# A hybrid attention and S5 step: x normed amid the modulation's loads, and more late turns behind the S5's first carries

## The chip, the cores and the metric

The kernel runs on one core of one Trainium2 chip. Its engines are TensorE (PE, with PEld for the loads of its weights), VectorE (DVE), ScalarE (ACT), GpSimd (POOL) and SyncE (SP), which issues nearly all DMA transfers. The metric is the time of one execution on the device in microseconds (us), less is better. Times of before and after are medians of several runs; a profile is one execution.

## The reference, cut to what matters

One layer works on 1024 prompt tokens and 64 sample tokens of width 1024, 1088 in all, in nine token tiles (eight of 128, one of 64). All is float32.

```
mod   = silu(c) @ w_mod + b_mod                    # c: prompt and sample row
shift, scale, gate = three parts of 1024 columns
h     = rms_norm(x, g_norm) * (1 + scale) + shift
z     = h @ w_in                                   # 4936 columns, split:
q, k, v, qi, ki, wi, ga, u, gs, ma, mb = split_cols(z)
o     = attention of q over the 256 keys that the indexer (qi, ki, wi) selects
y     = S5(u)                                      # complex diagonal scan + D skip
yg    = GLU(gelu(y) @ w_glu)
merged = sigmoid(ma) * ((o * silu(ga)) @ w_attn_proj)
       + sigmoid(mb) * ((yg * silu(gs)) @ w_ssm_proj)
out   = rms_norm(x + gate * (merged @ w_out), g_final)
```

Outputs are `out` for both, the new keys, values and indexer keys, and the S5's last states.

## The kernel before

Products in float32 accuracy are made of float32r halves: a value is cast to `hi` (ACT) and `lo = value - hi` is subtracted (POOL or DVE), and a product is hi·hi + hi·lo + lo·hi, three passes over eight blocks of 128 (`mm3`). `split` (L155) does this for weights that `load_split` loads through two `raw` buffers.

**The start.** silu(c) is turned to columns `scs`. Then the loop at L472 goes through w_mod's first 2048 columns: for each of eight row blocks `k` the tile of the scale half (`j` = 1) and of the shift half (`j` = 0), 128 x 1024 each, 512 KB. `wm` tiles and tiles of x (`load_x`, L459) share one tag with five buffers. `SPLITW` says for each of the sixteen tiles whether it is split (`s`: ACT casts, DVE subtracts, two products with the float32r pair `c4`) or taken in float32 (`d`: one product with `cz`); either way the stationary operand has four columns and the sums land in four partitions of PSUM. x0 is loaded before the last w tile (`X0` = 14), x1 behind it. The steps of the S5's parameters (`ssm_params`, small DVE work) are taken at `PARK`. Then the rows `mrow` are copied out, turned by PE into columns, and DVE forms `acol` (scale) and `shcol` (shift), L510 to L514. The weights `wA` of the first projection (264 columns: three indexer heads, the indexer's keys, its weights) follow in four pairs of row blocks.

`norm(t)` squares a tile of x on ACT with a row sum, POOL takes the power -1/2 (L530), and DVE or ACT scales the tile in place. It also loads x two tiles ahead. `turn_x` (L537) turns one or two tiles by PE into PSUM, applies `acol` and `shcol` on DVE (L552) or ACT (L555), casts to `hhi` on ACT (L558) and subtracts to `hlo` on POOL (L559). `GROUPS` says which tiles go together, `HALVES` how many half groups are turned at each step of the loop over nine tiles (L649), where `chunk_a(t)` projects tile t with `wA`, rotates on POOL (`do_rope`, L239 to L242), stores the indexer's keys and stacks them for the scores. Behind it wB is loaded and the scores, the top-k selection and the attention follow.

**Late work.** The remaining projections are one list of jobs (`products`), 128 columns of w_in each, in three chunks of tokens (`CH`); a job has nine steps. `late` is a generator of these steps, and `weave(main, fill, ratio)` takes `ratio` steps of it for each yield of another stage: the attention (1.15), the S5 (3.2), gelu (3.0). What is left is run behind gelu.

**The S5.** `ssm()` (L1454) yields behind each of its steps: the input products `ssm_in(q)` for four quarters, the scan on DVE, and then for each quarter `ssm_fix(q)` (DVE adds the carries to the quarter's states, L1424 to L1427, and copies them to `zq`, L1435), `ssm_out_tables(q + 1)` (POOL, PE and round trips through DRAM) and `ssm_out(q)` (PE, L1447 and L1448, stored to `y_d`). gelu reads `y_d`, and the GLU follows.

A list scheduler lays out the order within each engine: the program's order is the priority, and an instruction that its model of durations holds for not ready is passed by later ones that are. On the chip each engine and SP's queue run strictly in the order laid out.

Of the kernel before, what the change touches and what calls it, by code (L numbers as in the profile page):

```python
# [51 lines left out]
N_BR = (7, 3, 2)  # L52
R_ATT = 1.15
R_SSM = 3.2
N_GAP = 12
R_GEL = 3.0
N_ATT = 14
# [1 line left out]
QH = 5  # L59
VH = 0  # L60
ORDER = "ost"
GROUPS = ((1, 2), (3, 4), (5, 6), (7,), (8,))
HALVES = (2, 1, 1, 1, 1, 1, 1, 2, 0)
SA = (3, 6, 4, 8, 2, 7, 5)
SB = (6, 3, 4, 8, 5, 2, 7)
MB = 3
PARK = (1, 2, 3)
PAR0 = 2
OT = 5
RAW = 2  # L70
SPLITW = "sdsdsdsdsdsdsddd"
X0 = 14
MODD = (1, 1, 1, 0, 0, 0, 1, 0)
XS_ON = "dadddaddd"
ROPE_ON = {2: "p", 4: "p", 5: "d"}
# [8 lines left out]
def hybrid_step(ctx, tc, ins, outs):  # L84
# [24 lines left out]
    def tpb():  # L109
        return ps_tp.tile([P, 4, P], F32, tag="tp", name="tp")  # L110
# [4 lines left out]
    def big():  # L115
        return ps_big.tile([P, 1024], F32, tag="big", name="big")
# [66 lines left out]
    def load_tok(c0, n):  # L183
        w = tokp.tile([P, 2, KD, n], F32R, tag="wtok", name="wtok")
        src = w_in[:, c0:c0 + n].rearrange("(k p) c -> p k c", p=P)
        nk = 2 if n <= 264 else 1
        for k in range(0, KD, nk):
            load_split(w[:, 0, k:k + nk, :], w[:, 1, k:k + nk, :], src[:, k:k + nk, :])
        return w
# [251 lines left out]
    tp = tpb()  # L441
    pe.transpose(tp[:, 0, :16], crow[0:16], ident[:16, :16])
    for b in range(2):
        silu = act.activation(scs[:, :, b], tp[:, 0, 8 * b:8 * b + 8], AF.Silu)
    c4 = small.tile([P, KD, 4], F32R, name="c4")
    dve.tensor_copy(c4[:, :, 0:2], scs)
    c_rest = dve.tensor_tensor(c4[:, :, 2:4], scs, c4[:, :, 0:2].bitcast(F32), op=OP.subtract)

    def chain(*gens):
        for g in gens:  # L450
            yield from g

    def run(gen):
        for _ in gen:
            pass
# [3 lines left out]
    def load_x(t):  # L459

        xts[t] = sxp.tile([P, D], F32, tag="wm", name="xt", bufs=5)
        sync.dma_start(xts[t][:tok_tile(t)[1]], x_rows(t))


    cz = sxp.tile([P, KD, 4], F32, name="cz", bufs=1)
    pool.memset(cz, 0.0)
    dve.tensor_copy(cz[:, :, 0:2], scs)
    scr = rb.tile([P, 6, 512], F32, tag="t1", name="scr")
    params = ssm_params(ssu)
    next(params)  # L470
    mp = [big(), big()]
    for k in range(KD):  # L472
        for j in (1, 0):
            wm = sxp.tile([P, D], F32, tag="wm", name="wm", bufs=5)
            last_w = sync.dma_start(wm, w_mod[k * P:(k + 1) * P, j * D:(j + 1) * D])
            if SPLITW[(2 * k + 1 - j)] == "d":
                parts = [(cz, wm)]
            else:
                wmh = wpool.tile([P, D], F32R, tag="whi", name="wmh")
                wml = wpool.tile([P, D], F32R, tag="wlo", name="wml")  # L480
                with tc.issue_after(silu.ins), tc.issue_after(c_rest.ins):
                    act.copy(wmh, wm)
                    dve.tensor_tensor(wml, wm, wmh.bitcast(F32), op=OP.subtract)
                parts = [(c4, wmh), (c4, wml)]
            for i, (c, w) in enumerate(parts):
                for h in range(0, D, 512):
                    last_mm[0] = pe.matmul(mp[j][0:4, h:h + 512], c[:, k, :], w[:, h:h + 512],
                              start=(k == 0 and i == 0), stop=(k == KD - 1 and i == len(parts) - 1))
            if 2 * k + 1 - j == X0:
                load_x(0)  # L490
        if k in PARK:
            next(params)
    load_x(1)
    mrow_t = kv1.tile([4, 2, D], F32, tag="bz", name="mrow")
    mrow = [mrow_t[:, i] for i in range(2)]
    for j in (1, 0):
        act.copy(mrow[j][:, 0:512], mp[j][0:4, 0:512])
        dve.tensor_copy(mrow[j][:, 512:], mp[j][0:4, 512:])
    tp = tpb()
    with tc.issue_after(last_mm[0].ins):  # L500
        pe.transpose(tp[:, 1, :40], crow, ident[:40, :40])
    mcol = tp[:, 0, 0:64].rearrange("p (m b) -> p m b", b=4)
    for blk in [*range(8, 16), *range(8)]:
        pe.transpose(mcol[:, blk, :], mrow[blk // 8][:, (blk % 8) * P:(blk % 8 + 1) * P], ident[0:4, 0:4])
    ccol = sxp.tile([P, 3, KD], F32, name="ccol", bufs=1)
    dve.tensor_copy(ccol.rearrange("p a b -> p (a b)"), tp[:, 1, 16:40])
    mc = sxp.tile([P, 16, 4], F32, name="mc", bufs=1)
    dve.tensor_copy(mc, mcol)
    both_b = [ccol[:, i, :, None].to_broadcast([P, KD, 2]) for i in range(3)]
    dve.scalar_tensor_tensor(acol, mc[:, 8:16, 0:2], 1.0, mc[:, 8:16, 2:4], op0=OP.add, op1=OP.add)  # L510
    dve.tensor_tensor(acol, acol, both_b[1], op=OP.add)
    dve.tensor_tensor(acol, acol, both_b[2], op=OP.mult)
    dve.tensor_tensor(shcol, mc[:, 0:8, 0:2], mc[:, 0:8, 2:4], op=OP.add)
    dve.tensor_tensor(shcol, shcol, both_b[0], op=OP.add)  # L514

    with tc.issue_after(last_w.ins):
        wA = load_tok(C_QI + 320, 264)
        load_x(2)
        sync.dma_start(rope, ins["rope_tab"])


    def norm(t):
        nt = tok_tile(t)[1]
        if 0 < t and t + 2 < 9:
            load_x(t + 2)
        xt = xts[t]
        ss = sxp.tile([P, 3], F32, tag="ss", name="ss", bufs=4)
        act.activation(scr[:nt, 4:6].rearrange("p a b -> p (a b)"), xt[:nt], AF.Square, accum_out=ss[:nt, 0:1])
        dve.tensor_scalar(ss[:nt, 1:2], ss[:nt, 0:1], 1.0 / D, EPS, op0=OP.mult, op1=OP.add)
        pool.tensor_tensor(ss[:nt, 2:3], ss[:nt, 1:2], nhalf[:nt], op=OP.pow)  # L530
        if XS_ON[t] == "d":
            dve.tensor_scalar(xt[:nt], xt[:nt], ss[:nt, 2:3], None, op0=OP.mult)
        else:
            act.activation(xt[:nt], xt[:nt], AF.Copy, scale=ss[:nt, 2:3])


    def turn_x(ts):  # L537
# [103 lines left out]
            yield  # L641
    late = counted(products(jobs))
    chunks = [chunk_a(t) for t in range(9)]
    norm(0)
    run(turn_x((0,)))
    norm(1)
    norm(2)
    turns = chain(*[turn_x(g) for g in GROUPS])
    for t in range(9):  # L649
        if t >= PAR0:  # L650
            next(params, None)
        if t < 6:
            norm(t + 3)
        for _ in range(HALVES[t]):
            next(turns)
        next(chunks[t])
        if t:
            next(chunks[t - 1])
# [501 lines left out]
    def gates():  # L1160


        sel = small.tile([P, 2], F32, name="sel")
        for b in range(2):
            dve.tensor_reduce(sel[:, b:b + 1], ident.rearrange("p (g r) -> p g r", r=32)[:, :, b],
                              axis=mybir.AxisListType.X, op=OP.add)
        for h in range(2):
            cols = slice(2 * D + h * 512, 2 * D + h * 512 + 512)
            w = tokp.tile([P, KD, 544], F32, tag="wtok", name="gw")
            pool.memset(w[:, :, 512:], 0.0)  # L1170
            pool.tensor_copy(w[:, :, 512:514], scs)
            sync.dma_start(w[:, :, 0:512], w_mod[:, cols].rearrange("(k p) c -> p k c", p=P))
            yield
            ps = bank1()
            for k in range(KD):
                g = 32 * (k % 4)
                pe.matmul(ps[g:g + 32], w[:, k, 512:], w[:, k, 0:512], start=(k < 4), stop=(k >= 4), skip_group_check=True)
            r = wpool.tile([P, 528], F32, tag="raw", name="grow", bufs=RAW)[:, :512]
            act.copy(r, ps)
            yield  # L1180
            o = bank1()[0:2]
            pe.matmul(o, sel, r, start=True, stop=True)
            act.copy(r[0:2], o)
            bm = wpool.tile([P, 528], F32, tag="raw", name="gbias", bufs=RAW)[0:2, :512]
            sync.dma_start(bm, ins["b_mod"][:, cols].to_broadcast([2, 512]))
            pool.tensor_tensor(bm, r[0:2], bm, op=OP.add)
            sync.dma_start(gate_d[:, h * 512:h * 512 + 512], bm)
# [266 lines left out]
    def ssm():  # L1454
        for q in range(4):
            if q == 0:
                with tc.issue_after(last_mm[0].ins):
                    ssm_in(q)
            else:
                ssm_in(q)  # L1460
            yield
        for i, _ in enumerate(ssm_scan()):
            if i == OT:
                ssm_out_tables(0)
            yield
        for q in range(4):
            ssm_fix(q)
            yield
            if q < 3:
                ssm_out_tables(q + 1)  # L1470
                yield
            ssm_out(q)
            yield
# [228 lines left out]
```

## Time and profile before

| | us |
|---|---|
| three runs, median (lowest to highest) | 1055.84 (1055.79 to 1056.0) |
| the profiled execution | 1058.36 |
| its span, first to last instruction | 1056.6 |
| PE busy | 984.9 |
| DVE busy | 686.0 |
| ACT busy | 462.7 |
| POOL busy | 298.7 |

The span is what the trace covers; the execution's own time is 1.8 us longer. Busy times are sums over the whole span, of stages with different limits. The granted clock of TensorE, 0.968 of full speed on average, is given by stretch: 1.00 is 2.4 GHz, 0.50 is 1.2 GHz.

### The profile page before, as it was taken

The page shows a single profiled execution, that of the slowest core. Times are in us where ns is not written, and L with a number is a line of the kernel's source. Part 1 is how long each engine was busy: PE and PEld are TensorE (multiplying, and loading weights), DVE is VectorE, ACT ScalarE, POOL GpSimd, SP SyncE. Part 2 cuts the span into 40 slices and gives each one's busy share as a digit, 9 for nine tenths or more (in the row PEclk, how much of TensorE's full clock was granted, in tenths as well). Part 3 has the DMA queues.
Part 4 walks back from the last instruction along what each step waited for, and adds up shares of the span by engine and source line. Part 5 has one row for each costly group of instructions (what it writes and reads, how often), then busy time and mean ns, then how long its engine had stood idle before and what let it go on. Part 6 is the DMA issues. An engine that isn't in the chain of part 4 may idle for free. (4 is left out here: it accounts for less than half of the span.)

```text
span 1056.6 us, 16627 instructions
## 1 busy us (share of the span) xinstructions
PE 984.9 (93%) x5948; PEld 893.3 (85%) x5948; DVE 686.0 (65%) x1416; ACT 462.7 (44%) x978; POOL 298.7 (28%) x438
## 2 busy tenths in 40 slices
PE   7777999999899999999999996989979999999997
PEld 1466877998689999999898995879969999998786
DVE  5764898899787778866665999811034556664243
ACT  3574577321276566666625211111462344442122
POOL 2475102531622222112152387351114000001201
PEclk9797999999899999999999998899989999999999
DMA  8730301144332222112294241323733255534133
GB/s 294 230 94 24 91 1 48 44 162 147 83 73 60 59 60 59 51 55 65 60 135 117 83 119 35 85 59 89 189 115 97 83 165 159 161 108 160 50 136 115
DMA packets 137413, 106.18 MB, mean 100 GB/s; under 512 B 32638, under 2 KB 124328, under 8 KB 137328
## 3 DMA queue, kind: packets, MB, share of 16 engines
q1 hardware_dynamic: 135808, 102.82, 34.6%
q10 hardware_dynamic: 1232, 2.23, 0.6%
q8 instruction: 47, 0.77, 0.3%
q14 instruction: 38, 0.31, 0.1%
q0 software_dynamic: 288, 0.05, 0.0%
HBM read 77.79 MB, written 25.17 MB: 97 GB/s over the span
## 5 line engine op out<-in xcount | busy, mean ns | idle before, releaser
L201 PE MATMUL acc<-hhi,whi 128*128 128x384 f32 (+1 forms) x768 | 259.3, 342 | 13.3 <-ACT sg L627 7.4
L202 PE MATMUL acc<-hlo,whi 128*128 128x384 f32 (+1 forms) x768 | 254.3, 335 | 0.0
L157 POOL TENSOR_TENSOR wlo<-raw,whi 128x512 fp32r<-128x512 f32 x64 | 88.2, 1393 | 283.3 <-ACT whi L156 147.8
L201 PEld LDWEIGHTS acc<-hhi,whi 128*128 128x128 f32 x768 | 148.0, 193 | 18.6 <-ACT sg L627 8.0
L206 PE MATMUL acc<-hhi,wlo 128*128 128x384 f32 (+1 forms) x768 | 150.8, 334 | 0.0
L202 PEld LDWEIGHTS acc<-hlo,whi 128*128 128x128 f32 x768 | 148.1, 193 | 0.6
L206 PEld LDWEIGHTS acc<-hhi,wlo 128*128 128x128 f32 x768 | 129.6, 190 | 2.3 <-issue 1.6
L611 ACT COPY st<-acc 128x384 f32<-128x384 f32 (+1 forms) x60 | 27.7, 461 | 102.2 <-PE acc L206 101.7
L1075 DVE TENSOR_TENSOR pt<-tp,pt 128x512 fp32r<-128x512 f32 (+3 forms) x112 | 57.0, 518 | 17.6 <-ACT pt L1074 16.6
L1054 ACT ACTIVATE pm<-pm,mx 128x1024 f32<-128x1024 f32 (+8 forms) x72 | 56.1, 779 | 25.5 <-DVE mx L1047 25.1
L1074 ACT CAST pt<-tp 128x512 fp32r<-128x512 f32 (+3 forms) x112 | 49.3, 451 | 35.9 <-PE tp L1070 34.4
L1637 POOL TENSOR_TENSOR yh<-yh,gfin 128x512 f32<-128x512 f32 (+1 forms) x9 | 11.6, 1291 | 173.3 <-ACT xr L1633 173.3
L1047 DVE CUSTOM_DVE_ANT_0 pm<-sc,bias 128x512 f32<-128x512 f32 (+4 forms) x72 | 42.6, 593 | 26.9 <-PE sc L1044 26.3
L201 PE MATMUL acc<-wohi,mhi 128*128 128x512 f32 (+2 forms) x152 | 56.7, 377 | 0.0
L202 PE MATMUL acc<-wolo,mhi 128*128 128x512 f32 (+2 forms) x152 | 56.7, 377 | 0.0
L1070 PE MATMUL tp<-ident,pm 128*128 128x128 f32 (+2 forms) x328 | 52.8, 270 | 0.7 <-DVE pt L1075 0.6
L1044 PE MATMUL sc<-kst,qs 128*128 128x512 f32 (+3 forms) x192 | 52.0, 352 | 1.1 <-DVE mx L1047 0.5
L156 ACT CAST whi<-raw 128x512 fp32r<-128x512 f32 x64 | 37.8, 618 | 31.9 <-PE acc L202 18.4
L1087 PE MATMUL o<-pt,vst 128*128 128x256 f32 x288 | 47.5, 291 | 1.0 <-DVE pt L1075 1.0
L1070 PEld LDWEIGHTS tp<-ident,pm 128*128 128x128 f32 (+2 forms) x328 | 38.5, 139 | 9.8 <-DVE pt L1075 2.2
L706 DVE SCALAR_TENSOR_TENSOR sc<-relu,wi,sc 128x512 f32<-128x512 f32 (+5 forms) x42 | 42.6, 1017 | 3.8 <-ACT relu L704 1.0
L1087 PEld LDWEIGHTS o<-pt,vst 128*128 128x128 f32 x288 | 39.3, 188 | 4.4 <-DVE pt L1075 3.6
(493 smaller groups left out, 2244.8 us busy)
## 6 DMA issues: line engine op xcount, KB each, us to landing
raw<-in_w_in SPq DMA_DIRECT2D x68, 256.0 KB
wm<-in_w_mod SPq DMA_DIRECT2D x16, 512.0 KB
xt<-in_x_prompt SPq DMA_DIRECT2D x8, 512.0 KB
gw<-in_w_mod SPq DMA_DIRECT2D x2, 2048.0 KB
raw<-in_w_out SPq DMA_DIRECT2D x16, 256.0 KB
xr<-in_x_prompt SPq DMA_DIRECT2D x16, 256.0 KB
ma_d<-st SPq DMA_DIRECT2D x16, 192.0 KB
mb_d<-st SPq DMA_DIRECT2D x16, 192.0 KB
```

The lines of the kernel that those rows point to most:

```text
L157: rest_on[0].tensor_tensor(lo, raw, hi.bitcast(F32), op=OP.subtract)
L201: pe.matmul(ps, lhi(k), rhi(k), start=(k == 0), stop=False)
L202: pe.matmul(ps, lhi(k), rlo(k), start=False, stop=False)
L206: last_mm[0] = pe.matmul(ps, llo(k), rhi(k), start=False, stop=(k == nk - 1))
L706: dve.scalar_tensor_tensor(scores[b][:nq], r[:nq, :n], w, scores[b][:nq], op0=OP.mult, op1=OP.add, accum_out=sums[:nq, 0, col] if h == 4 e ...
L1044: pe.matmul(ps, self.st[:, self.h // 2, self.h % 2, :nq], self.keys[:, self.h // 4, j, c:c + m], start=(j == 0), stop=(j == 1))
L1047: dve.tensor_tensor_reduce(out=self.pm[:, c:c + m], in0=ps, in1=bias[self.b][:nq, c:c + m], op0=OP.add, op1=OP.min, scale=-0.125, scalar=t ...
L1054: act.activation(self.pm, self.pm, AF.Exp, bias=self.ng, scale=-1.0, accum_out=self.sm)
L1070: pe.transpose(tp[:rows, i, :nq], self.pm[:, c0:c0 + rows], ident[:nq, :nq])
L1074: act.copy(d0, tp[:rows, i0:i1, :nq])
L1075: dve.tensor_tensor(d1, tp[:rows, i0:i1, :nq], d0.bitcast(F32), op=OP.subtract)
L1087: last_mm[0] = pe.matmul(o, v[:rows, kt, pr // 2].rearrange("p a d -> p (a d)"), pk[:rows, j, i, :, :nq], start=(kt == 0 and j == 0), stop ...
```

## The change

The modulation's loop goes through all eight tiles of the scale half first, then through the shift half. No tile is split any more: each is taken in float32, with a stationary operand of 32 columns (`scp`), and row block k's sums go to PSUM partitions 32 (k mod 4) and on, so that there are four row groups; `mrow` has 128 partitions, and eight products with the selector `sel` per half (moved here from `gates`) add the groups and turn the rows to columns at once. `acol` is formed in the middle of the loads, `shcol` at the end.

x0 is loaded ahead of all w tiles, x1 to x3 behind w tiles 0, 1 and 2 (`XE`), and wA behind tile 12 (`WA_AT`). These four tiles are normed two tiles later and turned three tiles later, without modulation, into `hraw` (`turn_early`), which takes the buffers of the weights' halves. `mod_early` modulates them in place (per half tile three blocks on DVE, one on ACT), casts and subtracts. x4 to x8 are loaded behind the w tiles without any step of `norm` between, normed at `NORMS` and turned as before in `GROUPS` (4, 5), (6, 7), (8).

In the S5, `ssm_fix(0)` is followed by four yields instead of one (`N_FIX`), so that the weave takes 3 x 3.2 = 9.6 steps of `late` more there.

```diff
+N_FIX = (4, 1, 1, 1)
-GROUPS = ((1, 2), (3, 4), (5, 6), (7,), (8,))
-HALVES = (2, 1, 1, 1, 1, 1, 1, 2, 0)
+XE = (-1, 0, 1, 2)
+WA_AT = 12
+GROUPS = ((4, 5), (6, 7), (8,))
+NORMS = (2, 1, 1, 1, 0, 0, 0, 0, 0)
+HALVES = (0, 1, 1, 1, 1, 1, 1, 0, 0)
-PARK = (1, 2, 3)
+PARK = (3, 5, 7)
-SPLITW = "sdsdsdsdsdsdsddd"
-X0 = 14
...
-    for k in range(KD):
-        for j in (1, 0):
-            wm = sxp.tile([P, D], F32, tag="wm", name="wm", bufs=5)
-            last_w = sync.dma_start(wm, w_mod[k * P:(k + 1) * P, j * D:(j + 1) * D])
-            if SPLITW[(2 * k + 1 - j)] == "d":
-                parts = [(cz, wm)]
-            else:
...
+    hraw = [wpool.tile([P, KD, P], F32, tag=("whi", "wlo")[t % 2], name="hraw") for t in range(len(XE))]
+    def turn_early(t):
+        for k0 in (0, 4):
+            tp = tpb()
+            for i in range(4):
+                pe.transpose(tp[:, i, :], xts[t][:, (k0 + i) * P:(k0 + i + 1) * P], ident)
+            (act.copy if k0 else dve.tensor_copy)(hraw[t][:, k0:k0 + 4], tp)
+    def mod_early(t):
+        c = slice(t * P, (t + 1) * P)
+        for k0 in (0, 4):
+            ks = slice(k0, k0 + 4)
+            for k in range(k0, k0 + 4):
+                if k % 4 < 3:
+                    dve.tensor_scalar(hraw[t][:, k], hraw[t][:, k], acol[:, k, 0:1], shcol[:, k, 0:1],
+                                      op0=OP.mult, op1=OP.add)
+                else:
+                    act.activation(hraw[t][:, k], hraw[t][:, k], AF.Identity, bias=shcol[:, k, 0:1],
+                                   scale=acol[:, k, 0:1])
+            act.copy(hhi[:, ks, c], hraw[t][:, ks])
+            pool.tensor_tensor(hlo[:, ks, c], hraw[t][:, ks], hhi[:, ks, c].bitcast(F32), op=OP.subtract)
...
+    load_x(0)
+    mtp = bank1()
+    mcol = mtp[:, 0:32].rearrange("p (j k b) -> p j k b", j=2, b=2)
+    for n in range(2 * KD):
+        j, k = 1 - n // KD, n % KD
+        wm = sxp.tile([P, D], F32, tag="wm", name="wm", bufs=5)
+        last_w = sync.dma_start(wm, w_mod[k * P:(k + 1) * P, j * D:(j + 1) * D])
+        if n in XE[1:]:
+            load_x(XE.index(n))
+        if n == WA_AT:
+            wA = load_tok(C_QI + 320, 264)
+        g = 32 * (k % 4)
+        for h in range(0, D, 512):
+            last_mm[0] = pe.matmul(mp[j][g:g + 32, h:h + 512], scp[:, k, :], wm[:, h:h + 512],
+                                   start=(k < 4), stop=(k >= 4), skip_group_check=True)
+        if n in PARK:
+            next(params)
+        if n - 2 in XE:
+            norm(XE.index(n - 2))
+        if n - 3 in XE:
+            turn_early(XE.index(n - 3))
+        if k == KD - 1:
+            act.copy(mrow[:, j, 0:512], mp[j][:, 0:512])
+            dve.tensor_copy(mrow[:, j, 512:], mp[j][:, 512:])
...
+                for b in range(KD):
+                    pe.matmul(mcol[:, j, b, :], mrow[:, j, b * P:(b + 1) * P], sel, start=True, stop=True)
...
+    load_x(NE)
+    with tc.issue_after(last_w.ins):
+        load_x(NE + 1)
+        sync.dma_start(rope, ins["rope_tab"])
+        for t in range(NE + 2, 9):
+            load_x(t)
...
-    norm(0)
-    run(turn_x((0,)))
-    norm(1)
-    norm(2)
+    for t in range(2):
+        mod_early(t)
...
-        if t < 6:
-            norm(t + 3)
+        if t + 2 < NE:
+            mod_early(t + 2)
+        for _ in range(NORMS[t]):
+            norm(todo.pop(0))
...
             ssm_fix(q)
-            yield
+            for _ in range(N_FIX[q]):
+                yield
```

## Rows read from the trace of the kernel before

**Rows 1.** The page: busy time by engine (share of the span) x instructions.
```profile
PE 984.9 (93%) x5948; PEld 893.3 (85%) x5948; DVE 686.0 (65%) x1416; ACT 462.7 (44%) x978; POOL 298.7 (28%) x438
```

**Rows 2.** Stretches: length, each engine's busy time (x instructions), clock, DMA share, GB/s.
```profile
39.30:98.70 59.40, 44.17 (x296) 40.11 (x294) 32.20 (x69) 38.10 (x84) 43.71 (x148) 0.84 0.33 91
650.30:662.70 12.40, 0.07 (x2) 0.05 (x1) 12.31 (x14) 0.00 (x0) 10.06 (x7) 0.63 0.00 1
662.70:668.40 5.70, 5.70 (x31) 5.70 (x31) 5.63 (x12) 1.00 (x2) 0.00 (x0) 0.61 0.01 3
```

**Rows 3.** Stretches, a slice of the loads of w_mod; same columns.
```profile
20.00:30.00 10.00, 10.00 (x28) 1.26 (x27) 9.52 (x56) 2.30 (x4) 0.61 (x3) 1.00 0.94 342
```

**Rows 4.** Timeline, loads issued on SP: start, duration, engine, line, op, tiles, count.
```profile
1.54 22.78 SPq L475 DMA_DIRECT2D wm<-in_w_mod  x15
7.60 0.33 SPq L475 DMA_DIRECT2D wm<-in_w_mod  x1
27.01 0.33 SPq L475 DMA_DIRECT2D wm<-in_w_mod  x1
66.29 1.28 SPq L462 DMA_DIRECT2D xt<-in_x_sample  x1
```

**Rows 5.** Timeline, PE: one row group, turns, four row groups, the next product.
```profile
12.85 1.88 PE L487 MATMUL big<-wm,cz 128*4 128x512 f32 x4
38.96 1.92 PE L547 MATMUL big<-ident,xt 128*128 128x128 f32 x8 [0.48 <-ACT xt L534]
253.65 1.92 PE L1177 MATMUL tp<-gw 128*32 128x512 f32 x16
255.51 0.44 PE L201 MATMUL acc<-hhi,whi 128*128 128x384 f32 x1
```

**Rows 6.** Timeline, other engines of the start, up to the last rope.
```profile
5.27 1.04 ACT L482 CAST wmh<-wm 128x1024 fp32r<-128x1024 f32 x1 [2.00 <-DMA wm<-in_w_mod]
32.82 0.67 DVE L498 COPY mrow<-big 4x512 f32<-4x512 f32 x1
33.20 1.06 ACT L528 ACTIVATE scr<-xt 128x1024 f32<-128x1024 f32 x1
39.28 0.18 DVE L512 TENSOR_TENSOR acol<-acol,ccol 128x16 f32<-128x16 f32 x1
98.42 0.24 POOL L242 TENSOR_TENSOR zA<-rope,rope 64x32 f32<-64x32 f32 x1
```

**Rows 7.** Groups by line, POOL, 39.3 to 98.7: busy, mean ns | idle, releaser.
```profile
L530 POOL TENSOR_TENSOR ss<-ss,nhalf 128x1 f32<-128x1 f32 (+1 forms) x7 | 4.6, 658 | 6.4 <-DVE ss L529 6.4
L157 POOL TENSOR_TENSOR wtok<-raw,wtok 128x528 fp32r<-128x528 f32 x3 | 4.3, 1455 | 0.5 <-ACT wtok L156 0.5
```

**Rows 8.** Waits of PE: total, times, longest.
```profile
PE tp L1448 <- DVE zq L1435: 12.3, 1, 12.3
```

**Rows 9.** Timeline, PE: the product behind that wait.
```profile
662.65 0.82 PE L1448 MATMUL tp<-zq,cs 128*128 128x136 f32 x2 [12.33 <-DVE zq L1435]
```

**Rows 10.** Timeline, DVE: the same 544-wide form beside POOL's work and without it.
```profile
649.34 1.77 DVE L1424 TENSOR_TENSOR f<-car,arf 128x544 f32<-128x544 f32 x1
663.74 0.72 DVE L1424 TENSOR_TENSOR f<-car,arf 128x544 f32<-128x544 f32 x1
```

**Rows 11.** Timeline, ACT: evictions of one late job's three chunks.
```profile
735.40 0.49 ACT L627 ACTIVATE sg<-acc 128x384 f32<-128x384 f32 x1 [3.38 <-PE acc L206]
739.61 0.49 ACT L627 ACTIVATE sg<-acc 128x384 f32<-128x384 f32 x1 [3.72 <-PE acc L206]
743.13 0.44 ACT L627 ACTIVATE sg<-acc 128x320 f32<-128x320 f32 x1 [3.02 <-PE acc L206]
```

**Rows 12.** Timeline, POOL: a late job's product beside DVE.
```profile
672.05 1.44 POOL L620 TENSOR_TENSOR oT<-sg,oT 128x384 f32<-128x384 f32 x1 [11.29 <-ACT sg L619]
```

**Rows 13.** Timeline, the tail: the last gelu's rest, the last late chunk's eviction.
```profile
779.87 1.29 DVE L1503 TENSOR_TENSOR glo<-gt,ghi 128x1088 fp32r<-128x1088 f32 x1
807.75 0.43 ACT L611 COPY st<-acc 128x320 f32<-128x320 f32 x1
```

More of the change, by code (lines that the diff above doesn't have):

```diff
@@ L443, in hybrid_step @@
     for b in range(2):
[L444 to L447, printed above, removed]
+        act.activation(scs[:, :, b], tp[:, 0, 8 * b:8 * b + 8], AF.Silu)
     def chain(*gens):
@@ L462, in load_x @@
         sync.dma_start(xts[t][:tok_tile(t)[1]], x_rows(t))
[L465 to L471, printed above, removed]
-    for k in range(KD):
-        for j in (1, 0):
-            wm = sxp.tile([P, D], F32, tag="wm", name="wm", bufs=5)
-            last_w = sync.dma_start(wm, w_mod[k * P:(k + 1) * P, j * D:(j + 1) * D])
-            if SPLITW[(2 * k + 1 - j)] == "d":
-                parts = [(cz, wm)]
-            else:
[L479 to L519, printed above, removed]
     def norm(t):
         nt = tok_tile(t)[1]
-        if 0 < t and t + 2 < 9:
-            load_x(t + 2)
         xt = xts[t]
@@ new lines, in hybrid_step @@
+    scp = sxp.tile([P, KD, 32], F32, name="scp", bufs=1)
+    pool.memset(scp, 0.0)
+    dve.tensor_copy(scp[:, :, 0:2], scs)
+    sel = small.tile([P, 2], F32, name="sel")
+    for b in range(2):
+        dve.tensor_reduce(sel[:, b:b + 1], ident.rearrange("p (g r) -> p g r", r=32)[:, :, b],
+                          axis=mybir.AxisListType.X, op=OP.add)
+    scr = rb.tile([P, 6, 512], F32, tag="t1", name="scr")
+    params = ssm_params(ssu)
+    next(params)
+    load_x(0)
+    mp = [big(), big()]
@@ new lines, in hybrid_step @@
+    mrow = kv1.tile([P, 2, D], F32, tag="bz", name="mrow")
+    mtp = bank1()
[13 more added lines that the diff above has]
+        if n in PARK:
+            next(params)
+        if n - 2 in XE:
[5 more added lines that the diff above has]
+            dve.tensor_copy(mrow[:, j, 512:], mp[j][:, 512:])
+            with tc.issue_after(last_mm[0].ins):
+                if j:
+                    pe.transpose(mtp[:, 64:104], crow, ident[:40, :40])
+                for b in range(KD):
+                    pe.matmul(mcol[:, j, b, :], mrow[:, j, b * P:(b + 1) * P], sel, start=True, stop=True)
+            if j:
+                ccol = sxp.tile([P, 3, KD], F32, name="ccol", bufs=1)
+                dve.tensor_copy(ccol.rearrange("p a b -> p (a b)"), mtp[:, 80:104])
+                both_b = [ccol[:, i, :, None].to_broadcast([P, KD, 2]) for i in range(3)]
+                dve.scalar_tensor_tensor(acol, mcol[:, 1], 1.0, both_b[1], op0=OP.add, op1=OP.add)
+                dve.tensor_tensor(acol, acol, both_b[2], op=OP.mult)
+            else:
+                dve.tensor_tensor(shcol, mcol[:, 0], both_b[0], op=OP.add)
@@ L537, in turn_x @@
+    NE = len(XE)
+    load_x(NE)
[4 more added lines that the diff above has]
+            load_x(t)
     def turn_x(ts):
@@ L643, in hybrid_step @@
     chunks = [chunk_a(t) for t in range(9)]
-    norm(0)
-    run(turn_x((0,)))
-    norm(1)
-    norm(2)
+    for t in range(2):
+        mod_early(t)
     turns = chain(*[turn_x(g) for g in GROUPS])
+    todo = list(range(NE, 9))
     for t in range(9):
@@ L1160, in gates @@
     def gates():
[L1163 to L1166, printed above, removed]
         for h in range(2):
```

## The prediction

> **What bounds the kernel now.** I read the page's busy times first: TensorE (PE) is busy 93% of the span [rows 1], so only a stretch in which PE stands idle or runs at half clock can give much. The list of PE's waits and its timeline name the one large hole: 12.33 us up to 662.65, in which the S5's output products wait for DVE's carries [rows 8, 9]. The stretches, engine by engine [rows 2], show the other place: from 39.3 to 98.7, where x is normed, turned, modulated and first projected, PE is busy 44.2 of 59.4 us at a granted clock of 0.84, and no engine is full (POOL 43.7, the others less). Before 39.3 the modulation's products follow their loads. From 98.7 on PE is nearly dense, so time won ahead of it, or in the hole, moves the whole rest forward. The profiled execution took 1058.36 us, 1.8 more than its span; the three timed runs have a median of 1055.84, 2.5 below it. I make the sum as a difference on the profiled execution and take it off the median.
>
> **The start, until the shift column.** Four tiles of x enter the five buffers that w_mod's sixteen tiles run through: 20 loads up to the last w tile (17 before, where x0 stood ahead of it), and wA's four stand ahead of the last three.
> - Before, the sixth load was issued at 7.60 and the seventeenth at 27.01 [rows 4]: eleven intervals of 1.76 us. The wire's share of one is 0.52 MB at 342 GB/s [rows 3], 1.53. The twentieth is then issued at 7.60 + 14 x 1.53 to 1.76 = 29.0 to 32.2; wA's 1.08 MB (264 x 1024 x 4 B) adds 3.2 at that rate: 32.2 to 35.4.
> - Behind the last issue: 3.7 to land (issued 1.54, ACT released by it at 5.27 [rows 4, 6]), four float32 records 1.9 [rows 5], the PSUM copy 0.7 [rows 6], eight products with sel, one vector op 0.2. No row shows a sel product. The nearest are eight turns, 1.92 at half clock [rows 5]: bounds are half of it, 1.0, and twice it, 3.8 (two records each); I take 1.5, as they move two columns instead of 128. Sum 8.0: shift column at 40.2 to 43.4.
> - Holding: an x tile keeps its buffer through square 1.1, pow 0.7, scale 0.7, eight turns 1.9 and their copies 0.7 [rows 5 to 7] (the scale taken as the copy), 5.1 us against a w tile's 1.9. Four such over five buffers cost at most 4 x 3.2 / 5 = 2.5; I take half. Queued behind it: SP is a queue, so each w load stands behind the x load that waits for a buffer, and wA's third and fourth raw loads, which wait for ACT's and POOL's splits, hold the last three w loads; on PE the next w product stands behind turns whose tile is not yet scaled.
> - So 44.6, with bounds 39.7 (sel 1.0) and 49.9 (43.4 + 2.5 + 2.3 for dear sel products + 14 x 0.12, should each w tile cost PE its whole 1.88). Before it was 39.28 [rows 6]: the change costs 5 us here.
>
> Seven w tiles lose their split into two float32r halves, a cast of 1.04 on ACT [rows 6] and a subtraction on DVE, for which a w buffer and PE had waited; what that leaves free on both carries the four norms, hraw's copies and sel's two reductions. The four row groups: the same form in gates ran 16 records in 1.92 us against 4 in 1.88 for one group [rows 5], so PE stops setting the interval. The parameters stay at the same w tiles.
>
> A rule against it: the Trainium skill (TensorEngine Tiling (Array Packing), Key Properties) says that changing the tiling mode drains TensorE, and the new loop alternates narrow products with full-width turns. In the trace gates' sixteen narrow records run from 253.65 to 255.57 and the next full-width product starts at 255.51 [rows 5]: no drain is seen. By the rule some ten switches would each cost a fraction of a microsecond, by the row nothing; either lies inside the holding term.
>
> **The start, from the shift column to the last projected tile.** It lasted 59.4 us, to POOL's last rope at 98.66 [rows 6]. POOL's 43.7 in it lose three of wA's subtractions (3 x 1.46) and two pows (2 x 0.66) [rows 7], now done earlier: 38.0; its hlo subtractions, ropes and constants stay. 15.7 us of it were idle, behind casts and behind norms strung on late loads: the last x tile was issued at 66.29 [rows 4], because x tiles waited for buffers. After the change all five are free when x4 to x8 are wanted, and four tiles need only modulation, cast and subtraction. Lower bound: 38.0 + 2 to the first cast = 40. Upper: all idle time stays, 53.7. I take 46, half the idle time, since cast and subtraction still alternate half tile by half tile.
> So 44.6 + 46 = 90.6 against 98.7: -8.1, with bounds -19.0 (39.7 + 40) and +4.9 (49.9 + 53.7). What is late next: wB's loads, which stand on SP behind the last key store; they move along.
>
> **The S5.** Three yields more at 3.2 steps each put 9.6 steps of the late projections between the first carries and the first output products. A chunk's pace is 4.21 us at 384 columns and 3.52 at 320 [rows 11], a job of nine steps 11.9: 1.33 a step, 12.7 for 9.6. Their weights come by loads that nothing in the hole delays. The hole is 12.3 [rows 8]. The output products behind it ran 5.7 us at clock 0.61 [rows 2]; at full clock 3.5, so 2.2 more.
> Against: a job's splits and products come along on POOL, 2 x 1.46 [rows 7] and 3 x 1.44 [rows 12], 7.2 us. DVE's 544-wide ops took 0.72 where POOL stood idle and 1.77 where it was busy 10 of 12.4 us [rows 2, 10], so up to 7.2 x 0.59 = 4.2 us of delay for the carries, of which the fill's excess covers 0.4. Gain between 14.5 and 10.7; I take 12. It is zero if the turns don't go there. What the late work covers later is thinner: its last chunk is evicted at 807.75, the last gelu's rest ends at 781.2 [rows 13], so 26 us of it lie behind gelu, of which 12.7 are taken; the cover holds.
>
> **Sum.** -8.1 - 12 = -20.1: 1038.3 for a profiled execution, 1035.7 against the median.
>
> **Rivals.**
> 1. The start gives nothing: POOL's idle time stays, since cast and subtraction follow each other through one tile at a time (for it: POOL idles 15.7 us with much of its data on chip). Then 44.6 + 53.7 = 98.3, -0.4, and only the S5 counts: 1043.4. Against: a good part of that idle time ended with late norms. Chance 0.17.
> 2. The S5's gain is given back in the tail, where gelu then sets the end of the stage. For: ACT evicts late chunks behind gelus that wait for their loads. Against: the 26 us of cover. Then -8.1 alone: 1047.7. Chance 0.08.
> 3. Slower: the five buffers starve the loads. Every w load stands in SP's queue behind x tiles that give their buffer back only when PE, in order, has turned them, and PE stands behind w products that wait for loads. Price: 14 us for each microsecond of interval. All gains outside it are 13.4 (59.4 - 46) + 12 = 25.4, so it decides from a shift column at 64.7, which is an interval of 3.3 (18.8 + 14 x 3.3). At 3.6 the column comes at 69.2 and the kernel takes 1055.8 + 29.9 - 25.4 = 1060.3. Against: 1.76 was kept while ACT and DVE split w tiles. Chance 0.06.
> 4. No change: the order within each queue is laid out anew, and a hole as long opens elsewhere. 1055, chance 0.04.
>
> **How the numbers follow.** The forecast has 0.65 and a range of its own of 1025 to 1045. To hold 0.8 the range takes in rivals 1 and 2 and both bounds of the start: 1022.3 (-19.0 - 14.5) to 1052 (+4.9 with 8.7 left of the S5's gain). 0.2%, about what a measurement can tell from no change, is 2.1 us. Faster: forecast and rivals 1 and 2, 0.90, less a little for their mixtures, 0.89; same 0.04; slower 0.07.
>
> **What the profile after would show.** Loads: w's last issue near 35 and the shift column's vector op near 44; past 50 the holding term failed. POOL's last rope near 91, its idle time between shift column and that near 8, and all x loads issued by 50. In the S5: PE's wait for zq under 4 us, the clock there full, late products between. In the tail: the last late chunk evicted near 788, still behind the last gelu. A wait for gelu ahead of the GLU's products would make rival 2 right, w loads more than 3 us apart rival 3; a stage of 54 us behind the shift column rival 1.

## The result, and the profile after

The changed kernel takes 1043.01 us (median of 4 runs, 1042.34 to 1043.72) beside 1055.82 for the kernel before; the ratio is 0.9887 [0.9864, 0.9909]. That is 12.8 us faster, where 20.1 were forecast. The time lies inside the range, but it is made up otherwise than forecast: the new start loses time, and the S5's turns gain nearly twice what they were given. The profiled execution took 1043.72 us with a span of 1041.9; PE is busy for 982.1 of it (before: 984.9 [rows 1]).

The waits of TensorE (PE) after: total, times, longest. L469, L527 and so on are lines of the changed file, some 20 beyond those of before.

```profile
PE big L527 <- DVE par L367: 8.2, 1, 8.2
PE big L571 <- DVE xt L472: 6.6, 3, 4.2
PE tp L613 <- POOL zA L244: 6.4, 3, 4.1
PE tp L1469 <- DVE zq L1456: 5.5, 1, 5.5
```

The 12.3 us in front of the S5's output products [rows 8] are gone, and 5.5 stand in front of the second quarter's. New are 8.2 us in front of the first product of the modulation and 6.6 for the scaled tiles of x; 4.1 of the 6.4 us for zA are one wait near the end of the start (before it was 3.9).

**The start.** The timeline of the changed kernel: ScalarE (ACT) and PE ahead of the first product, two loads of w_mod on SP (the sixth of the loads that share the five buffers, and the last), the products with the last tile, and the ends of the two stages that the forecast dated.

```profile
0.74 1.28 ACT L468 ACT_TABLE_LOAD   x1 [0.74 <-PEq L1711]
5.18 1.06 ACT L468 ACTIVATE scr<-xt 128x1024 f32<-128x1024 f32 x1 [3.16 <-DMA xt<-in_x_prompt]
8.02 1.06 ACT L468 ACTIVATE scr<-xt 128x1024 f32<-128x1024 f32 x1 [1.70 <-DMA xt<-in_x_prompt]
9.19 1.28 ACT L446 ACT_TABLE_LOAD   x1
10.48 0.25 ACT L446 ACTIVATE scs<-tp 128x8 f32<-128x8 f32 x2
11.07 1.93 PE L527 MATMUL big<-wm,scp 128*32 128x512 f32 x4 [8.17 <-DVE par L367]
...
14.72 0.34 SPq L520 DMA_DIRECT2D wm<-in_w_mod  x1
...
40.54 0.33 SPq L520 DMA_DIRECT2D wm<-in_w_mod  x1
...
46.29 1.90 PE L527 MATMUL big<-wm,scp 128*32 128x512 f32 x4 [0.29 <-DMA wm<-in_w_mod]
51.05 0.17 DVE L550 TENSOR_TENSOR shcol<-tp,ccol 128x16 f32<-128x16 f32 x1 [1.50 <-PE tp L542]
106.28 0.24 POOL L244 TENSOR_TENSOR zA<-rope,rope 64x32 f32<-64x32 f32 x1
109.83 0.80 PE L718 MATMUL big<-kis,qsa 128*128 128x512 f32 x1
```

And the row of before that answers to the last one, the first product of the index scores:

```profile
102.50 0.80 PE L693 MATMUL big<-kis,qsa 128*128 128x512 f32 x1
```

ACT's queue has the squares of x0 and x1, each waiting for its tile, and a second table load ahead of silu, though the code has silu first. So the first product with w_mod, which needs scp, DVE's copy of silu's output, starts at 11.07 (the lists name a neighbour of that copy on DVE, par), and by then the five buffers have long been full: no load of w_mod is issued until 14.72 (before: 7.60 [rows 4]). The shift column comes at 51.05 (before the last of these vector operations was at 39.28 [rows 6]), the last rope ends at 106.5 (98.66), and the first product of the index scores moves from 102.50 to 109.83: the start is 7.3 us longer.

Stretches after, answering to [rows 2]: shift column to last rope, the time in which the hole was, and 15 us of the carries behind it.

```profile
51.20:106.50 55.30, 40.74 (x272) 38.83 (x272) 32.12 (x78) 32.22 (x73) 38.94 (x145) 0.82 0.21 46
656.60:668.40 11.80, 11.80 (x77) 11.35 (x77) 11.64 (x17) 2.80 (x6) 7.16 (x9) 1.00 0.14 32
672.00:687.00 15.00, 15.00 (x104) 14.55 (x103) 14.90 (x13) 4.52 (x9) 14.69 (x10) 1.00 0.49 105
```

POOL is idle for 16.4 us of the first stretch (55.30 - 38.94); it was 15.7 of 59.4, and 8 were forecast. In the second PE is full at clock 1.00, where it had stood and then run at 0.61. In the third POOL and DVE are both full, and DVE's 544-wide operations behave as in [rows 10], 1.95 us there against 0.72 beside the idle POOL. The last row is the first of the second quarter's copies to zq:

```profile
673.60 1.93 DVE L1445 TENSOR_TENSOR f<-car,arf 128x544 f32<-128x544 f32 x1
678.21 1.95 DVE L1447 TENSOR_TENSOR zs<-zs,f 128x544 f32<-128x544 f32 x1
695.01 0.72 DVE L1448 TENSOR_TENSOR zs<-zs,f 128x544 f32<-128x544 f32 x1
695.99 0.42 DVE L1456 COPY zq<-zs 64x544 f32<-64x544 f32 x1
```

PE waits for these copies until 697.37. The second quarter's carries are added by 673.7, and PE has used the first quarter's zq by 674.7, but on DVE's queue the copies stand behind the sixteen 544-wide operations of the last two quarters (673.60 to 695.73). The order is the same before (there the copies start at 681.41), but no wait of PE hangs on it. So the new wait of 5.5 us needs both the order and the slow operations; at 0.72 each the sixteen would take some 10 us less, by these rows. No run moves the copies.

**The S5 and the tail.** The same work on PE, from the S5's first products to the first of the GLU, before, after, and in the kernel that has the turns alone (one row of each kernel; same columns):

```profile
556.00:808.00 252.00, 225.51 (x1426) 219.51 (x1427) 131.64 (x195) 74.72 (x136) 94.49 (x82) 0.94 0.37 97
```

```profile
563.50:791.00 227.50, 218.49 (x1426) 213.37 (x1427) 135.11 (x195) 71.16 (x132) 98.16 (x82) 0.98 0.40 107
```

```profile
557.00:783.50 226.50, 218.27 (x1425) 213.14 (x1426) 134.21 (x195) 70.90 (x132) 98.98 (x82) 0.98 0.40 107
```

Before, PE was idle for 26.5 us of it, with the turns alone for 8.2: 18.3 less. With as many records (1426, 1425) it is busy for 7.2 us less, since the mean clock rises from 0.94 to 0.98. The hole gives only 7.4 of this (12.3 less the 4.9 us that open at the second quarter). 7.4 more are two waits in the tail, 4.25 and 3.13 us, that stood in the trace of before and are gone. 3.0 more are waits for the tables that POOL computes (ca): 4.3 us in two waits before, 1.3 with the turns. PE's waits before (first two rows) and with the turns alone:

```profile
PE acc L201 <- ACT sg L627: 7.4, 2, 4.3
PE tp L1334 <- POOL ca L1325: 3.1, 1, 3.1
PE tp L1449 <- DVE zq L1436: 4.9, 1, 4.9
PE tp L1335 <- POOL ca L1326: 1.3, 1, 1.3
```

ACT's timeline of before shows what the waits in the tail were, and that of the kernel with the turns what took their place:

```profile
764.99 1.28 ACT L1500 ACT_TABLE_LOAD   x1 [4.17 <-DMA yt<-y_d]
...
770.64 1.28 ACT L627 ACT_TABLE_LOAD   x1
771.94 0.49 ACT L627 ACTIVATE sg<-acc 128x384 f32<-128x384 f32 x1
772.33 1.13 ACT L156 CAST whi<-raw 128x512 fp32r<-128x512 f32 x2
773.47 1.28 ACT L1500 ACT_TABLE_LOAD   x1
```

```profile
764.68 2.35 ACT L1502 ACTIVATE gt<-yt 128x1024 f32<-128x1024 f32 x1
...
766.93 0.54 ACT L612 COPY st<-acc 128x384 f32<-128x384 f32 x1
```

Before, the gelus met the silu gates of the late projections. The first gelu waited 4.17 us for its load at the head of ACT's queue, a pair of gelus with its table load took 5.6 us (764.99 to 770.64), and each change between gelu and silu cost a table load of 1.28; the evictions (sg) and the weight casts that PE needs stood behind all of it. Ten steps later in the sequence the gelus meet copies, and no table load stands between them.

The last late chunk is now evicted at 790.81 (788 forecast), and the last gelu's rest ends at 783.1, so the late work still covers it:

```profile
781.77 1.29 DVE L1525 TENSOR_TENSOR glo<-gt,ghi 128x1088 fp32r<-128x1088 f32 x1
790.81 0.43 ACT L635 COPY st<-acc 128x320 f32<-128x320 f32 x1
```

**The output projection.** One loss lies where nothing was changed. Its 456 products follow each other without a gap in both kernels, from 951.1 to 1048.0 before and from 933.7 to 1033.3 after, 96.9 and 99.6 us, both at clock 1.00 (first and last start of a third of them, min/median/max ns):

```profile
L201 PE MATMUL acc<-wohi,mhi x152: 276/389/397, 951.1 to 1048.0; 128*128 128x512 f32 x128, 128*64 128x256 f32 x16, 128*64 128x512 f32 x8
```

```profile
L203 PE MATMUL acc<-wohi,mhi x152: 279/392/398, 933.7 to 1033.3; 128*128 128x512 f32 x128, 128*64 128x256 f32 x16, 128*64 128x512 f32 x8
```

### The profile page after: what moved, and what is told of

It is laid out like the page before. It is cut to its first block, busy times and chain, and to the rows that moved or that the text cites. A ratio compares the mean times of both kernels' runs of the same rounds, so it can differ in the third digit from the quotient of the medians.

```text
span 1041.9 us, 16650 instructions
## 1 busy us (share of the span) xinstructions
PE 982.1 (94%) x5964; PEld 894.3 (86%) x5964; DVE 683.4 (66%) x1420; ACT 454.1 (44%) x971; POOL 302.8 (29%) x440
## 5 line engine op out<-in xcount | busy, mean ns | idle before, releaser
L203 PE MATMUL acc<-hhi,whi 128*128 128x384 f32 (+1 forms) x768 | 256.1, 338 | 6.6 <-ACT whi L158 6.5
L159 POOL TENSOR_TENSOR wlo<-raw,whi 128x512 fp32r<-128x512 f32 x64 | 90.5, 1427 | 276.4 <-ACT whi L158 137.1
L203 PEld LDWEIGHTS acc<-hhi,whi 128*128 128x128 f32 x768 | 145.9, 190 | 11.8 <-ACT whi L158 8.6
L204 PEld LDWEIGHTS acc<-hlo,whi 128*128 128x128 f32 x768 | 145.9, 190 | 0.6
L1069 PE MATMUL sc<-kst,qs 128*128 128x512 f32 (+3 forms) x192 | 51.9, 352 | 1.0 <-DVE mx L1072 0.6
```

Of the source, the lines that this page charges most:

```text
L159: rest_on[0].tensor_tensor(lo, raw, hi.bitcast(F32), op=OP.subtract)
L203: pe.matmul(ps, lhi(k), rhi(k), start=(k == 0), stop=False)
L204: pe.matmul(ps, lhi(k), rlo(k), start=False, stop=False)
L1069: pe.matmul(ps, self.st[:, self.h // 2, self.h % 2, :nq], self.keys[:, self.h // 4, j, c:c + m], start=(j == 0), stop=(j == 1))
```

## Experiments

The medians below are each beside runs of the kernel before on the same chip; the ratio with its 95% interval is to those. Two variants are compared by their medians; those runs of the kernel before had medians between 1053.95 and 1055.82, so a difference between variants of different groups is good to some 2 us.

**Which part does what.** The two parts alone: the S5's turns in the kernel before, and the changed kernel without them.

```
s5_only (the kernel before)       start_only (the changed kernel)
+N_FIX = (4, 1, 1, 1)             -N_FIX = (4, 1, 1, 1)
             ssm_fix(q)           +N_FIX = (1, 1, 1, 1)
-            yield
+            for _ in range(N_FIX[q]):
+                yield
```

> The kernel before with the S5's three turns alone. Theory from the two traces: these turns gain more than the 12 us of the forecast, since the stalls behind the gelus in the tail and the half clock around both go with the hole: 20 to 23 us, 1033 to 1036, below the full change. Rival, the forecast's own term: 12 us, 1044, and the whole change stands at 1043 because the start gave nothing.

> The full change without the S5's turns, so the new start alone. Theory: it costs 7 us (shift column at 51 instead of 39.3, first scores product at 110 instead of 102.5), so 1062 to 1064, slower than before. Rival, the forecast: it gains 8, 1047.7, and the S5 gained only 5. Second rival: it changes nothing, 1055.

s5_only: 1031.74, ratio 0.9788 [0.9765, 0.9811], 22.3 us faster than the 1054.06 beside it. start_only: 1063.5, ratio 1.0086 [1.0062, 1.011], 9.4 us slower. The product of the two ratios is 0.9872, the whole change's 0.9887: the parts add. The forecast's split (-8.1 and -12) is refuted, and with it the first rival, by which the start would give nothing.

**What the start loses.** Two edits of the changed kernel that only move instructions: the first on ACT and a few small ones on DVE, the second on POOL alone; every other queue keeps its order.

```
silu_first
-        act.activation(scs[:, :, b], ..., AF.Silu)
+        silu = act.activation(scs[:, :, b], ..., AF.Silu)
-        act.activation(scr[:nt, 4:6]..., xt[:nt], AF.Square, ...)
+        with tc.issue_after(silu.ins): act.activation(scr[:nt, 4:6]..., xt[:nt], AF.Square, ...)
const_late    (rope_a: POOL's last rope of the last projected tile)
-    topk_constants()
+    with tc.issue_after(rope_a.ins): topk_constants()
```

> The full change with the norms' squares put behind silu on ScalarE's queue; one activation table then serves both. Theory: the squares of x0 and x1 and the second table load ahead of silu are what holds the first w product until 11.07, with the five buffers full and no w load issued until 14.7; with silu first the product starts near 6, the shift column comes 4 to 5 us sooner (46 to 47) and the kernel takes 1037.5 to 1039.5. Rival: the buffers held by x tiles and the raw loads of wA set the pace; the first product comes sooner but the shift column stays at 50 to 51, and the time within 1 us of 1043.

> The full change with the 69 small memsets of the top-k constants put behind the last rope on GpSimd instead of ahead of the last three chunks' ropes. Theory: they cost the end of the start 4 to 5 us (TensorE stands 4.06 us at 99.10 for a rope behind them, with chunk 8's products queued behind that wait): last rope near 102, first scores product near 105.5, 1038 to 1039.5. Rival: TensorE would then wait for chunk 8's modulation or for wB instead, and the time stays within 1 us of 1043.

silu_first: 1038.2, ratio 0.9846 [0.9822, 0.987], 4.8 us below the change's 1043.0. Its timeline has one table load instead of two, and the first product 4.5 us sooner; the shift column follows by 4.0, the first scores product by 4.8 (105.04). The column's place is known to some 3 us only: in three traces with the same loads and the old order on ACT it starts at 50.39, 51.05 and 53.26 (start_only, the change, const_late); in the two with silu first at 47.01 and 46.41.

```profile
0.74 1.28 ACT L446 ACT_TABLE_LOAD   x1 [0.74 <-PEq L1711]
2.94 0.25 ACT L446 ACTIVATE scs<-tp 128x8 f32<-128x8 f32 x2 [0.92 <-PE tp L444]
6.59 1.89 PE L527 MATMUL big<-wm,scp 128*32 128x512 f32 x2 [3.69 <-DVE ss L469]
47.01 0.17 DVE L550 TENSOR_TENSOR shcol<-tp,ccol 128x16 f32<-128x16 f32 x1 [1.31 <-PE tp L542]
```

const_late: 1036.1, ratio 0.9821 [0.9797, 0.9846], 6.9 us below the change, more than expected. The 4.06 us wait is gone from PE's list, and the last rope ends 48.0 us behind the shift column (53.44 to 101.44) instead of 55.3. POOL is idle for 13.0 of them:

```profile
PE tp L613 <- POOL zA L244: 2.4, 2, 1.6
```

```profile
53.44:101.44 48.00, 36.87 (x272) 35.34 (x272) 32.18 (x77) 32.26 (x73) 35.00 (x58) 0.93 0.27 54
```

In the changed kernel those memsets ran from 93.2 to 97.8 on POOL, 89 of them at 0.09 us (not 69, as the expectation has it), ahead of the last three chunks' ropes; the turn of zA that waits for such a rope stood on PE ahead of chunk 8's products, and so chunk 8's own rope came late as well.

**Is the new start worth something without these two?** The old start and the new one, both with late constants, and the new with silu first.

```
s5_const    s5_only and the edit of const_late
after_both  the edits of silu_first and const_late
```

> The old start with the S5's turns, and the top-k constants' memsets put behind the last rope. Theory: the memsets stand ahead of the last ropes in the old start too (TensorE waits 3.87 us there, at 97.5), but chunk 8's products are done by then, so less hangs on them: 2.5 to 4 us, 1028 to 1029.5 against the 1031.7 with the turns alone. Rival: only the new order pays for the memsets, and the time stays at 1031 to 1032.5.

> The full change with silu first and the constants late together. Theory: the two losses lie one behind the other, so they add: 1043 - 4.8 - 6.9 = 1031.3 (1030 to 1032.5), shift column near 47, last rope near 96: about 3 us behind the old start with late constants, since 2.1 MB more (three tiles of x more, four raw loads of wA half ahead) still pass before the shift column. Rival, the forecast: without these two accidents the new start is 8 us faster than the old one, 1021 to 1024.

s5_const: 1028.74, ratio 0.9767 [0.9751, 0.9783]; it is the fastest kernel of the study, and ahead of the changed kernel by 1.2%. after_both: 1032.11, ratio 0.9805 [0.9787, 0.9823]; the two losses add, as expected. The first scores product is at 97.81 in the old start and at 97.89 in the new: freed of both, the new start brings nothing. Its shift column comes 7.9 us later (46.59 against 38.74), and the stage behind is 7.8 us shorter. Of that POOL's work is 4.7 us less (39.7 to 35.0), its idle time 3 (16 to 13).

```profile
97.81 0.80 PE L694 MATMUL big<-kis,qsa 128*128 128x512 f32 x1
```

```profile
97.89 0.50 PE L718 MATMUL big<-kis,qsa 128*128 128x512 f32 x1
```

**Where the S5's 22 us come from.** Ten steps moved within the kernel, so that the tail changes and the hole doesn't, and the other way round.

```
gap22 (the kernel before)    gap2_fix4 (s5_only)
-N_GAP = 12                  -N_GAP = 12
+N_GAP = 22                  +N_GAP = 2
```

> The kernel before with ten late steps more ahead of the S5 and none more in the hole. Theory: about half of the 22 us came from the tail, where silu's evictions and weight casts stood on ScalarE behind gelus that wait for their loads (TensorE 4.25 and 3.13 us, half clock around); the same ten steps taken from there without filling the hole give 7 to 11 us: 1043 to 1047, with the 12.3 us hole still in the trace. Rival: all of it is the hole's, the stalls in the tail follow from it: 1053 to 1056.

> The turns of the change with ten late steps fewer ahead of the S5, so the hole is filled and the tail meets the same late products as before. Theory: 11 to 15 us of the 22 are left, 1039 to 1043, with the stalls behind gelus back. Rival: the hole alone gives everything, 1031 to 1033. Third possibility: fewer steps ahead of the S5 open a wait in front of its first products, which would show there.

gap22: 1045.53, ratio 0.9923 [0.9905, 0.9941], 8.4 us faster with the hole still there, even longer, and no row for sg among PE's waits:

```profile
PE tp L1448 <- DVE zq L1435: 14.3, 1, 14.3
PE acc L201 <- ACT whi L156: 9.5, 4, 5.2
```

gap2_fix4: 1053.15, ratio 0.9994 [0.9982, 1.0005], no gain; 11 to 15 us were expected. The waits behind the gelus are back, and with fewer steps ahead of it the S5's first products wait for DVE:

```profile
PE acc L202 <- ACT sg L628: 6.4, 2, 4.2
PE tp L1371 <- DVE eb L278: 4.0, 2, 3.0
```

Each variant pays a bill that the change doesn't: gap22 2 us more of hole and a new wait of 3.1 for a weight cast in front of the S5, gap2_fix4 some 5 us in front of the S5's products. With these set aside, moving the tail is worth some 13 us and filling the hole some 6. That is near the 22 together, but an estimate from two unlike traces. The waits for ca follow the ten steps too, not the hole: they are 1.3 us in gap22, with the hole still there, and 4.3 in gap2_fix4. What stands is that the hole gives less than half: 7.4 us of idle time, and at most the 2.2 of half clock behind it, of the 25.5 between the stretches of before and s5_only (the profiled executions differ by 24.2, the medians by 22.3); and gap22's 8.4 came without it.

**The pace of the output projection.** c4, which the change takes away, was 128 bytes a partition in the first pool of SBUF's left side; in the built programs what lies above it there, w_out's halves too, lies 128 bytes lower after the change, and the right side (mhi, mlo) where it was.

```
after_pad (the changed kernel)          both_pad416 (after_both)
+    pad = small.tile([P, 32], F32)     +    pad = small.tile([P, 104], F32)
```

> The full change with an unused tile of 128 bytes a partition allocated where before c4 lay; no instruction is added and every engine's order stays. The output projection takes 2.7 us longer in all kernels with the new start (first to last product 99.97 us against 97.28 in before), with the same 456 products back to back: 233 ns against 227 each. Theory: with c4 gone everything on the left side of SBUF lies 128 bytes lower, w_out's halves with it, and the pace of these products depends on where they lie; the tile restores the 97.3 us and the kernel takes 1040.0 to 1041. Rival: the pace follows from something else that the new start left behind; 1042.5 to 1043.5 and 99.97 us.

> The kernel with silu first and late constants, and an unused tile of 416 bytes a partition: w_out's halves then lie 288 bytes above their place in before, at multiples of 1024 bytes, where the 128-byte tile put them back to it. Theory: place and pace are bound to each other, and only the 128 bytes below were bad; the output projection takes 97.3 us or less and the kernel 1029 to 1030, as fast as the old start with the S5's turns and late constants (1028.7) within its interval: with its three accidents taken away the new start is worth nothing here. Rival: every place but the old one is slow, 99.97 us and 1032.1. Second rival, the forecast's 8 us for the new start: 1021 to 1024.

after_pad: 1040.74, ratio 0.9862 [0.9845, 0.9879], 2.3 us below the change, and the products are back at 96.9 us with every instruction in its old place in the queues. both_pad416: 1033.15, ratio 0.9799 [0.9777, 0.9822], 99.6 us and no gain: 288 bytes above the old place the products are as slow as 128 below, so the theory's second half falls. By an estimate, after_both's 1032.1 less the 2.7 of the slow products, the new start would stand at 1029.4, beside the 1028.7 of the old; no run shows it.

```profile
L203 PE MATMUL acc<-wohi,mhi x152: 276/389/398, 932.4 to 1029.3; 128*128 128x512 f32 x128, 128*64 128x256 f32 x16, 128*64 128x512 f32 x8
```

```profile
L203 PE MATMUL acc<-wohi,mhi x152: 278/393/397, 921.7 to 1021.3; 128*128 128x512 f32 x128, 128*64 128x256 f32 x16, 128*64 128x512 f32 x8
```

**Two attempts to shorten the new start**, both on after_both:

```
both_norm                                       both_wa_late
+    norm(4); norm(5)                                    if n == WA_AT:
     for t in range(2): mod_early(t)            -            wA = load_tok(C_QI + 320, 264)
-NORMS = (2, 1, 1, 1, 0, 0, 0, 0, 0)            +            with tc.issue_after(last_w.ins): wA = load_tok(...)
+NORMS = (0, 1, 1, 1, 0, 0, 0, 0, 0)            -WA_AT = 12
                                                +WA_AT = 15
```

> The kernel with silu first and late constants, and besides x4 and x5 normed before the first two tiles' modulation instead of behind it. Theory: behind the shift column TensorE waits 3.4 to 4.9 us for x4's scale, which stands on VectorE behind 18 modulations in place (0.5 us each) though x4 has landed; with the norm ahead that wait goes and the first scores product comes 3 to 4 us sooner (94 to 95), 1028 to 1029.5. Rival: modulation, cast and subtraction set the pace anyway and the wait moves to them: within 1 us of 1032.1.

> The kernel with silu first and late constants, and wA's four raw loads put behind w_mod's last load (before: two of them at 3.8 us, two ahead of the last three w tiles). Theory: what stands ahead of the shift column is a sum of bytes; 1.08 MB less brings it from 46.6 to 43 or 44, but the first projections then wait for wA's splits, so the first scores product moves by less than 1.5 us either way: 1030.5 to 1033.5. Rival: the raw loads fill time in which the five buffers are held anyway, and the column stays within 1 us of 46.6.

both_norm: 1033.83, ratio 0.9799 [0.9783, 0.9815], no gain, a miss. The waits for scaled x shrink from 5.8 to 4.3 us, those for the ropes of zA grow from 2.6 to 7.0. both_wa_late: 1037.18, ratio 0.9825 [0.9807, 0.9843], 5.1 us slower by the medians, some 2 by the ratios. The shift column comes at 44.3, 2.3 us sooner, less than the spread of single traces above, so what wA's bytes cost it is not settled. Behind it wA is late: its last split on POOL ends at 55.6 instead of 40.0, the first products with hlo start at 56.5 instead of 51.9, and the first scores product moves from 97.9 to 101.4, more than expected.

## Why the prediction was right and where it was wrong

**The shift column at 44.6** was wrong by 6.6 us (51.2). The step that failed is the first of its sum: it took the sixth load at before's 7.60, that is, it took the chain ahead of the first product (crow, silu, scp) as unchanged, and did not ask what the new norms put in front of silu on ACT. The sixth load went out at 14.72, 7.1 later; with silu first it goes out at 10.21, and the column comes 4.0 sooner. The interval and the holding, for which the forecast set its sign "past 50", did not fail: the fourteen intervals with wA's share took 25.8 us, where 29.1 were taken (14 x 1.76, 3.2 for wA, 1.25 for holding). What stands behind the last issue was 2.7 longer, 10.7 instead of 8.0: the last tile took 5.7 us to land instead of 3.7, the products with sel 2.14 instead of 1.5. The last load of w_mod went out at 40.5, not near 35; the x loads were all issued by 48.3, as forecast.

**The stage of 46 us behind it** was wrong by 9.3 us, and with its bounds (40 to 53.7). The step that failed is the one on POOL's idle time: of 15.7 us half was to go. POOL's work came out as summed, 38.9 us instead of 38.0, and 16.4 stayed idle. That is what rival 1 said, and the sign that the forecast gave for it, a stage of 54 us, was there (55.3). Part of the idle time hangs on the top-k constants, which "stay": they were counted as busy time of POOL and not as a block ahead of the last ropes. With them out of the way the stage takes 48.0, 7.3 us less (6.5 between silu_first and after_both), about half of it work and half idle time. But the 48 is near the forecast's 46 by luck: the memsets' work is no longer in it, and 13.0 us are idle, not 8. That the old start pays for the same memsets (3.0 us between the medians of s5_only and s5_const) was to be read in before's trace, where PE waited 3.9 us at 97.5 for the rope behind them. The change made it dearer, because chunk 8's products now stood behind that wait.

**The gain of the start, -8.1,** was so a loss of 9.4 in the kernel's time: 7.3 at the first scores product, 2.7 in the output projection, which the forecast didn't look at. The two mechanisms themselves have the signs that the forecast gave them, a later column (+5) and a shorter stage (-13.4); measured without the two losses they are +7.9 and -7.8, and cancel.

**The S5's -12** had its mechanism right: the turns go into the hole, PE runs there at full clock, and DVE slows beside POOL. That slowing came out past the dear end: with the order on DVE's queue, which the forecast didn't read, it opens a hole of 5 us at the second quarter, where 4.2 us in all were the limit given. The term that was mis-sized is the tail, put at nothing. "The cover holds" asked only whether a loss would come; that 7.4 us of waits and some half-clock time already stood in the tail's trace, and would go when other late products meet the gelus, was not priced. s5_only's stretch shows 18.3 us less idle time, of it 7.4 in the hole and 10.4 in these waits and those for ca, and 7.2 us less busy time at the higher clock.

**The rivals.** The first came nearest in time (1043.4). Its mechanism for the stage held, POOL's idle time stayed; but the start doesn't give nothing, it loses, and the S5 gave more than it was given. The second expected the tail to take back what it in fact added to. Of the third the mechanism was there in small, late loads through full buffers, from a queue that it didn't name (ACT instead of SP). The time of 1043 lies in the range because two errors, 17.5 us in the start and 10 in the S5, have opposite signs.

**What was weighed against it:** by the Trainium skill (TensorEngine Tiling (Array Packing), Key Properties) changing the tiling mode drains TensorE; the forecast took the row instead, no drain. The timeline of the changed kernel has two such changes in a row, each group starting no later than the one before it ends (27.45 + 1.92 = 29.37, 29.30 + 0.55 = 29.85). No drain shows, but the ends of products are modelled in these profiles, so one of about a tenth of a microsecond would not be seen:

```profile
27.45 1.92 PE L527 MATMUL big<-wm,scp 128*32 128x512 f32 x8
29.30 0.55 PE L483 MATMUL tp<-ident,xt 128*128 128x128 f32 x3
29.78 3.26 PE L527 MATMUL big<-wm,scp 128*32 128x512 f32 x8
```

## What to carry to other kernels

Where a change puts new work on an engine's queue, read that queue's order ahead of the first instruction on which the stage hangs, and price small instructions by their place in the queue and not by their busy time. Where it takes work out of a stretch, look there for waits that already stand in the trace: moving late products can cure a stall as well as uncover one. When a fill lets an engine come sooner, read what the next thing it needs stands behind on the queue that makes it. Test a change's parts alone: here one of them alone beats the whole, and more so with one block of memsets moved.

## What was unexpected of the hardware

The pace of a dense run of float32r products can depend on where tiles lie in SBUF: with the same instructions in the same order, at clock 1.00 and without waits, 456 products take 96.9 us from the first start to the last with the left side's tiles, w_out's halves among them, at the old place, 99.6 at 128 bytes lower and 99.6 at 288 bytes higher. All fourteen traces agree, six at the old place and eight at the others. Which of the moved tiles matters, and which rule is behind it, the runs don't show.

At the start the loads moved more than the 342 GB/s that the forecast worked with: from 5 to 10 us the trace of the changed kernel shows 406 (that of before had 393 there), and from 45 to 50:

```profile
45.00:50.00 5.00, 4.03 (x17) 1.58 (x16) 0.69 (x1) 1.63 (x3) 0.00 (x0) 1.00 1.03 409
```
